# A hybrid encoder step in fp32: the embedding's input turned by VectorE ahead of time and kept in memory in two parts, and the embedding weight's parts kept too

## The chip, the cores and the metric

The kernel runs on one core of one Trainium2 chip. The metric is the device time of one execution in microseconds; lower is better. The engines named below are TensorE (PE in the profile: matmuls; PEld: its weight loads), VectorE (DVE), ScalarE (ACT), GpSimd (POOL) and SyncE (SP). SyncE computes nothing and issues most DMAs; GpSimd and ScalarE issue some as well. Each of these queues issues its DMAs in the order in which they stand in it.

## The reference, cut to what matters

One layer is applied to 2048 prompt rows and 32 sample rows of width 1024. First a mixer: RMSNorm, an input projection to 3072 columns, a short convolution and a pooling, and an output projection that is added to `h`. Then the per-layer embedding, which this change is about:

```python
    h = h + jnp.concatenate([yA, yB], axis=-1) @ w_out
    gate = jax.nn.sigmoid(rmsnorm(h, g_ple) @ w_ple_gate)
    h = h + (p @ w_ple) * gate
```

`p` is 2080 x 256 and `w_ple` 256 x 1024. A final RMSNorm closes the step. Everything is float32.

## The kernel before, in words

**Products in two parts.** A float32 operand is split by `split` (L77 to L80): ScalarE rounds it to the type fp32r (the high part, a CAST in the profile at L78) and VectorE subtracts that from the operand (the low part, L79). A product is then three matmuls: high by high, high by low, low by high. Most projections save one product in eight by Strassen's scheme on 2 x 2 blocks (`seven`).

**Stages.** The rows are cut into five blocks of 416, in three groups: blocks 0 and 1, 2 and 3, and block 4 with the 32 sample rows at its end.

1. The input projection runs over the groups (`GROUPS`), and in each over four units (j = 0 to 3; one unit has 128 channels of each kind). In the second group (profile: about 232 to 428 us) a unit is `Unit.seven`: 21 half products of 12 matmuls, each with weights that are loaded raw by SP, combined by VectorE and split by ScalarE and VectorE (`pair_weights`). Between the half products the unit calls `aside()`, 24 times in a unit. From unit 1 of the second group on, `aside` steps the generator `last_block`, which prepares the rows of the third group: SP loads them to a slot of the pool `xin` (five slots), VectorE scales them, POOL's queue stores them, SP loads them back in another order, VectorE turns them in 32 x 32 blocks in place (`turned_in_place`, L1112), and they are split and stored in `b_d` by POOL's queue. `at_pace(steps, num, den)` lets num of den calls of `aside` advance the generator by one step; `last_block` is stepped at 1 in 3.
2. At the end of the third group, `early_embedding` splits the embedding's weight (`embedding_weights`) and, after the group, the embedding's first three tiles (`EARLY`) are multiplied (about 540 to 549 us).
3. The output projection over pairs of 128-row tiles (about 549 to 711 us), with x added; `h` goes to memory (`h_d`).
4. The embedding `p @ w_ple` for the other tiles but one (about 711 to 751 us); its rows go to memory (`e_d`). Meanwhile the gate's weights are loaded (`wg_r`) and combined and split.
5. The gate projection over pairs of tiles (about 751 us to the end), with the product by the gate and the final norm. The last pair (`last_pair`) multiplies the embedding of the last tile itself.

**The embedding before the change.** Its input must stand with the 256 channels on the partitions. `embed` (L105 to L151) has `prep(c)` for tile c of its list and `run(c)`. For every fourth tile `prep` loads up to four tiles of `p` with one SP DMA (L122, sample rows L125). For each tile two TensorE transposes against the identity (L131) go to a PSUM bank, and `split` (L133) makes the parts `pps`. `run(c)` calls `prep` for c, c + 1 and c + 2, then does 12 matmuls of 512 columns (`embed_product`, L103), two ScalarE copies to the output tile (L148) and an SP store (L149). The slots of `pps` are four of the pool `st`, which the carried sums of the projections use as well. The weight's parts for stage 4 come from `embedding_chunks`: SP loads a chunk, ScalarE and VectorE split it into slots of the pool `cmb` (eight slots, shared with the frames of the output projection). `last_pair` does the same for its tile and weight (L1432, L1446).

**What sets the order.** The framework schedules: it walks the program with estimated costs and fixes each engine's and each queue's order; instructions with `keep_in_program_order` keep their place. On the chip each engine and each DMA queue then runs its list in order and waits on semaphores.

## Time and profile before

| | |
|---|---|
| median of 3 runs | 927.13 us (925.54 to 928.31) |
| profiled execution | 927.1 us |
| its span, first to last instruction | 925.3 us |
| TensorE busy | 907.0 us (98%), 4479 matmuls |
| VectorE busy | 722.8 us (78%) |
| ScalarE busy | 476.2 us (51%) |
| mean TensorE clock granted | 0.994 |
| moved by DMA | 186.37 MB, 201 GB/s over the span |

How to read the profile: a group line gives source line, engine, operation, output and inputs by the program's names, the shape, the count, then the busy time, the mean duration of one in ns, the idle time of the engine just before them and what ended it. A matmul's duration runs on into the next one, so the cost of a matmul on TensorE's path is the distance between starts. In the timeline a row gives the start and the length in us; rows of one kind that follow each other are merged and counted. "SPq" is SP's DMA queue.

### The profile page before, as it was taken

How to read it: one execution, taken by the hardware profiler on the slowest of the kernel's cores; microseconds unless marked ns; L12 is line 12 of the kernel's file. 1: busy time of each engine (PE TensorE's matmuls, PEld its weight loads, DVE VectorE, ACT ScalarE, POOL GpSimd, SP SyncE). 2: the span in 40 equal slices, each digit the busy share in tenths (PEclk: the TensorE clock that was granted, in tenths of full speed). 3: DMA queues.
4: the chain of work that ended last, by engine and by line, in shares of the span. 5: the costliest groups of instructions: out<-in, count | busy, mean ns of one | idle time of the engine just before them, and what ended most of it. 6: DMA issues, size and time to landing. Idle time of an engine off the chain costs nothing. (4 is left out here: it accounts for less than half of the span.)

```text
span 925.3 us, 12917 instructions
## 1 busy us (share of the span) xinstructions
PE 907.0 (98%) x4479; PEld 819.9 (89%) x4479; DVE 722.8 (78%) x1225; ACT 476.2 (51%) x880; POOL 152.8 (17%) x276
## 2 busy tenths in 40 slices
PE   7999999999999999999999999999999999999996
PEld 5999999999999999999999987888877868888884
DVE  6896898999488989785777679665554799888965
ACT  6744556554345455443545456334334776565554
POOL 3110222312001111000000010111111002333324
PEclk8999999999999999999999999999999999999998
DMA  8345555859955646357755359756775886799882
GB/s 245 87 152 153 167 160 178 265 154 317 411 165 174 191 155 189 100 180 277 201 169 173 125 192 289 263 186 177 251 220 167 292 259 160 190 232 232 227 240 91
DMA packets 140654, 186.37 MB, mean 201 GB/s; under 512 B 12044, under 2 KB 111244, under 8 KB 139309
## 3 DMA queue, kind: packets, MB, share of 16 engines
q1 hardware_dynamic: 120093, 126.07, 44.4%
q0 software_dynamic: 17760, 53.97, 19.8%
q10 hardware_dynamic: 2736, 5.51, 1.8%
q8 instruction: 35, 0.57, 0.3%
q14 instruction: 30, 0.25, 0.1%
HBM read 128.93 MB, written 56.56 MB: 200 GB/s over the span
## 5 line engine op out<-in xcount | busy, mean ns | idle before, releaser
L78 ACT CAST y_S<-y_fS 128x512 fp32r<-128x512 f32 x32 | 19.5, 621 | 41.9 <-PE x_o L168 18.9
L103 PE MATMUL e<-wq,pps 128*128 128x512 f32 (+1 forms) x156 | 38.9, 399 | 0.2 <-ACT pps L78 0.2
L168 PE MATMUL x_o<-wo_b,y_S 128*128 128x512 f32 x128 | 35.8, 391 | 0.0
L168 PE MATMUL x_g<-wg_b,g_S 128*128 128x512 f32 x128 | 35.7, 389 | 0.0
L564 PE MATMUL x_zbv<-B,w_zbv_S 128*128 128x416 f32 x168 | 34.2, 352 | 0.0
L564 PE MATMUL x_zab<-B,w_zab_S 128*128 128x416 f32 x168 | 34.1, 351 | 0.0
L564 PE MATMUL x_ch<-B,w_ch_S 128*128 128x416 f32 x168 | 34.1, 351 | 0.0
L564 PE MATMUL z_zab<-B,w_zab_S 128*128 128x416 f32 x168 | 34.0, 351 | 0.0
L564 PE MATMUL z_zbv<-B,w_zbv_S 128*128 128x416 f32 x168 | 34.0, 351 | 0.0
L564 PE MATMUL z_ch<-B,w_ch_S 128*128 128x416 f32 x168 | 34.0, 350 | 0.0
L103 PEld LDWEIGHTS e<-wq,pps 128*128 128x128 f32 (+1 forms) x156 | 27.4, 182 | 6.9 <-ACT pps L78 0.5
L1391 POOL DMA_DIRECT2D e<-h_d x28 | 24.8, 907 | 52.3 <-DVE e L1388 45.3
L70 POOL TENSOR_SCALAR ms_x<-ssq_x 128x1 f32<-128x1 f32 (+2 forms) x18 | 10.7, 592 | 127.5 <-ACT junk L89 127.2
L564 PEld LDWEIGHTS z_zbv<-B,w_zbv_S 128*128 128x128 f32 x168 | 31.4, 188 | 0.3
L564 PEld LDWEIGHTS z_zab<-B,w_zab_S 128*128 128x128 f32 x168 | 31.4, 188 | 0.3
L564 PEld LDWEIGHTS z_ch<-B,w_ch_S 128*128 128x128 f32 x168 | 31.4, 188 | 0.3
L564 PEld LDWEIGHTS x_zab<-B,w_zab_S 128*128 128x128 f32 x168 | 31.3, 188 | 0.4
L564 PEld LDWEIGHTS x_ch<-B,w_ch_S 128*128 128x128 f32 x168 | 31.3, 188 | 0.3
L564 PEld LDWEIGHTS x_zbv<-B,w_zbv_S 128*128 128x128 f32 x168 | 31.3, 188 | 0.4
L78 ACT CAST y<-y 128x512 fp32r<-128x512 f32 x24 | 14.8, 619 | 29.6 <-PE x_o L168 14.0
L168 PEld LDWEIGHTS x_o<-wo_b,y_S 128*128 128x128 f32 x128 | 23.9, 188 | 5.2 <-ACT c_o L1194 0.3
L168 PEld LDWEIGHTS x_g<-wg_b,g_S 128*128 128x128 f32 x128 | 24.0, 188 | 5.0
(582 smaller groups left out, 2649.9 us busy)
## 6 DMA issues: line engine op xcount, KB each, us to landing
y<-y_d SPq DMA_DIRECT2D x16, 512.0 KB, 6.3
x<-in_x_prompt_dram SPq DMA_DIRECT2D x16, 512.0 KB, 5.5
h_d<-x SPq DMA_DIRECT2D x16, 512.0 KB, 2.6
hn<-h_d SPq DMA_DIRECT2D x61, 128.0 KB, 6.7
xt<-in_x_prompt_dram SPq DMA_DIRECT2D x15, 512.0 KB, 7.4
e<-e_d SPq DMA_DIRECT2D x15, 512.0 KB, 5.9
e<-h_d POOLq DMA_DIRECT2D x28, 256.0 KB, 6.8
out_dram<-e POOLq DMA_DIRECT2D x14, 512.0 KB, 3.9
```

The lines of the kernel that those rows point to most:

```text
L70: nc.gpsimd.tensor_scalar(ms[:n], ssq[:n], scalar1=1.0 / D, scalar2=EPS, op0=ALU.mult, op1=ALU.add)
L78: ins = nc.scalar.copy(hi, src)
L103: nc.tensor.matmul(ps[:n], pps[:, a, k, :n], wp[k][b][:, cs], start=k + q == 0, stop=k == 1 and q == 2)
L168: nc.tensor.matmul(ps[:n], lhs[:, k, a, :n], w[b][:, k], start=start and k + q == 0, stop=k == KH - 1 and q == 2, skip_group_check=True)
L564: nc.tensor.matmul(ps[:, :NB], lhs[:, k, x], b[:, k, y], start=start and k + q == 0, stop=stop and k == KH - 1 and q == 2, skip_group_chec ...
L1391: nc.gpsimd.dma_start(ee, h_d[r:r + P, at[1] * NH:at[1] * NH + NH], accum_op=ALU.add)
```

## The change

The input `p` of the embedding is no longer turned by TensorE where it is used. A new generator, `p_steps`, does it in the second group, from unit 1 on, with the same means as `last_block`: SP loads four tiles in a block order (four DMAs, 64 channels each, in pieces of 256 bytes) to a slot of `xin`; VectorE turns them in place in 32 x 32 blocks; for each tile ScalarE and VectorE make the two parts, and POOL's queue stores them to `pt_d` (256 KB a tile). It is stepped at 23 in 68 calls of `aside`, beside `last_block`. Turning by blocks puts channels in another order on the partitions, so the rows of `w_ple` are loaded in the same order (four DMAs of 32 rows for each of two chunks). The weight's parts are stored once, at the end of the third group, to `wp_d`, and are loaded from there for stage 4 and the last pair; there they were split anew from the raw weight. `prep` in `embed` now only loads `pps` from `pt_d`, a tile at a time, and the transposes, the PSUM bank and the splits there are gone, in `last_pair` too.

```diff
+    pt_d = [tc.dram_tile([P, 2, 2, P], F32, name=f"pt_d{i}") for i in range(NT)]
+    wp_d = [[tc.dram_tile([P, D], F32, name=f"wp_d{k}{h}") for h in range(2)] for k in range(2)]
...
+    def p_load(pps, i):
+        n = tiles[i][1]
+        nc.sync.dma_start(pps.bitcast(F32)[:, :, :, :n], pt_d[i][:, :, :, :n])
...
-            pt = got["p"][:, (c % 4) * PLE:(c % 4 + 1) * PLE]
             pps = ring("pps", i)
-            ptp = tbank(f"ptp_{i}")
-            for k in range(2):
-                nc.tensor.transpose(ptp[:, k * P:k * P + n], pt[:n, k * P:(k + 1) * P], ident[:n, :n])
-            v = ptp.rearrange("p (k t) -> p k t", k=4)[:, :2, :n]
-            split(pps[:, 0, :, :n], pps[:, 1, :, :n], v)
+            p_load(pps, i)
...
-                nc.sync.dma_start(raw, w_ple[k * P:(k + 1) * P])
+                for q in range(4):
+                    nc.sync.dma_start(raw[q * 32:q * 32 + 32], w_ple[q * 64 + k * 32:q * 64 + k * 32 + 32])
                 t = [wtile(f"{name}{k}_{h}").rearrange("p k h n -> p (k h n)") for h in range(2)]
                 split(t[0], t[1], raw)
+                for h in range(2):
+                    nc.gpsimd.dma_start(wp_d[k][h], t[h].bitcast(F32))
...
+        def p_steps():
+
+            def load(c):
+                r, g = c * 4 * P, 16 if c < 4 else 1
+                t = ring4(xin, f"pc_{c}")[:, :g * 64]
+                for q in range(4):
+                    src = (p_p[r:r + 4 * P] if c < 4 else p_s)[:, q * 64:q * 64 + 64]
+                    nc.sync.dma_start(t[q * 32:q * 32 + 32].rearrange("p (g c) -> p g c", c=64),
+                                      src.rearrange("(g p) c -> p g c", p=32))
+                return t
+
+            t = load(0)
+            yield
+            for c in range(5):
+                tc.keep_in_program_order(nc.vector.transpose(t, t))
+                u = t.rearrange("p (g k t) -> p g k t", k=2, t=32)
+                yield
+                for m in range(4 if c < 4 else 1):
+                    i = c * 4 + m
+                    n = tiles[i][1]
+                    g = n // 32
+                    pps = pps_tile(i)
+                    v = lambda a: pps[:, a, :, :n].rearrange("p k (g t) -> p k g t", t=32)
+                    tc.keep_in_program_order(split(v(0), v(1), u[:, m * 4:m * 4 + g]))
+                    nc.gpsimd.dma_start(pt_d[i][:, :, :, :n], pps.bitcast(F32)[:, :, :, :n])
+                    if m == 0 and c < 4:
+                        t = load(c + 1)
+                    yield
...
-                        aside = at_pace(last_block(), 1, 3)
+                        paces = at_pace(last_block(), 1, 3), at_pace(p_steps(), 23, 68)
+                        aside = lambda: [pace() for pace in paces]
...
-        def embedding_chunks(name, rings=(ya, ya)):
+        def embedding_chunks(name):
...
-                raw = ring4(rings[k], f"{name}r_{k}")
-                nc.sync.dma_start(raw, w_ple[k * P:(k + 1) * P])
                 t = [cmb.tile([P, KH, 2, P], F32R, tag="c", name=f"{name}_{k}_{h}").rearrange("p a b c -> p (a b c)")
                      for h in range(2)]
-                split(t[0], t[1], raw)
+                for h in range(2):
+                    nc.sync.dma_start(t[h].bitcast(F32), wp_d[k][h])
...
-            pt = ss.tile([P, NH], F32, tag="s", name="p_l")[:, :PLE]
-            nc.sync.dma_start(pt, p_p[(i + 1) * P:(i + 2) * P])
+            pps = ss.tile([P, 2, 2, P], F32R, tag="s", name="pps_l")
+            p_load(pps, i + 1)
             e = load_rows(ya, "e", i, e_d)
-            wp = embedding_chunks("wl", (xh, qa))
+            wp = embedding_chunks("wl")
```

19 lines of the change are left out of this document (1 added, 18 removed).

## The prediction

> **What bounds the kernel now.** I read the page's engine line first, then the waits of TensorE, then windows by stage, then the timeline around the work that goes. The page and, under it, TensorE's waits (who, for whom, us in total, times, longest):
>
> ```profile
> PE 907.0 (98%) x4479; PEld 819.9 (89%) x4479; DVE 722.8 (78%) x1225; ACT 476.2 (51%) x880; POOL 152.8 (17%) x276
> ...
> PE pt L416 <- DVE xt L407: 3.2, 2, 2.3
> PE x_zab L564 <- DVE U L874: 0.3, 1, 0.3
> PE e L103 <- ACT pps L78: 0.2, 1, 0.2
> ```
>
> TensorE is busy 907.0 of 925.3 us, and its waits are small and mostly at the start. A matmul fewer is time gained, unless a neighbour becomes late. Which neighbour is near its limit is read by stage (length, busy time per engine with counts, clock, DMA share, GB/s): three units of the second group, the quiet end of the first projection, the embedding.
>
> ```profile
> 281.40:330.70 49.30, 49.01 (x260) 48.18 (x260) 43.68 (x78) 25.46 (x45) 7.32 (x11) 1.00 0.55 170
> 330.70:379.40 48.70, 48.70 (x259) 48.19 (x258) 44.80 (x75) 24.59 (x43) 5.78 (x7) 1.00 0.50 153
> 379.40:428.10 48.70, 48.70 (x259) 48.20 (x259) 36.19 (x60) 21.65 (x39) 2.89 (x4) 1.00 0.67 217
> 705.00:710.00 5.00, 5.00 (x24) 4.14 (x23) 1.38 (x2) 0.75 (x1) 0.00 (x0) 1.00 0.09 30
> 711.00:751.00 40.00, 39.76 (x190) 30.95 (x189) 28.59 (x52) 31.68 (x68) 1.06 (x3) 1.00 0.82 289
> ```
>
> The reader is to see that the change takes work from a stage whose second limit is DMA (0.82) and gives work to one whose second limit is VectorE (44.80 of 48.70 us).
>
> **What goes from TensorE.** There are 17 pairs of transposes, one pair a tile: 16 under L131, one under L1446. The groups and the timeline (start, length, engine, line, operation; in brackets the wait before it):
>
> ```profile
> L131 PE MATMUL ptp<-ident,ep 128*128 128x128 f32 (+1 forms) x32 | 5.7, 269 | 0.0
> ...
> 705.56 2.88 PE L168 MATMUL z_o<-wo_d,y_S 128*128 128x512 f32 x12
> 708.28 2.89 PE L168 MATMUL x_o<-wo_T,y 128*128 128x512 f32 x12
> 711.00 0.60 PE L131 MATMUL ptp<-ident,ep 128*128 128x128 f32 x4
> 711.84 0.96 PE L103 MATMUL e<-wq,pps 128*128 128x512 f32 x3 [0.24 <-ACT pps L78]
> 717.95 0.38 PE L131 MATMUL ptp<-ident,ep 128*128 128x128 f32 x2
> 718.08 3.00 PE L103 MATMUL e<-wq,pps 128*128 128x512 f32 x12
> 720.92 0.38 PE L131 MATMUL ptp<-ident,ep 128*128 128x128 f32 x2
> 721.06 3.00 PE L103 MATMUL e<-wq,pps 128*128 128x512 f32 x12
> ```
>
> A matmul's own duration overlaps the next one, so I go by starts. Twelve matmuls of 512 columns alone take 708.28 - 705.56 = 2.72 us. A tile of the embedding, twelve such and one pair, takes 721.06 - 718.08 = 2.98. A pair therefore costs 0.26 us of the path, and 17 pairs 4.4. At the start of the stage the four transposes and the wait for their copies take 711.84 - 711.00 = 0.84 us, of which two pairs are counted as 0.52; the other 0.3 goes too if the first tiles are there by 711. Gain: 4.7 us. Its bounds: 34 times the (0.60 - 0.27) / 3 = 0.11 between the starts of the four at 711.00 gives 3.7; 34 times the mean duration of 269 ns gives 9.1, excluded as an expectation by the 0.26 for a whole pair.
>
> On transposes the Trainium skill (TensorE: Matmul & The Clock Gate, Part 4: PE-mode transpose) gives about 275 ns in one kernel's context. By that as a cost on the path the gain would be an estimated 34 x 0.275 = 9.4 us; the trace agrees with it as a duration (269 ns), and not as a pitch.
>
> **What comes to the second group.** Five loads of 4 strided DMAs each on SP (20 issues), five VectorE transposes, 17 casts, 17 subtractions and 17 stores on POOL's queue, spread over 71 of the 72 steps of units 1 to 3. The nearest rows:
>
> ```profile
> L1112 DVE STREAM_TRANSPOSE xb<-xb x4: 433/1232/1234, 303.6 to 380.2; 128x1024 f32<-128x1024 f32 x3, 128x256 f32<-128x256 f32 x1
> L78 ACT CAST pps<-ptp 128x256 fp32r<-128x256 f32 (+1 forms) x16 | 5.7, 370 | 1.0 <-PE ptp L131 1.0
> L79 DVE TENSOR_TENSOR pps<-ptp,pps 128x256 fp32r<-128x256 f32 (+1 forms) x16 | 6.3, 407 | 3.2 <-ACT pps L78 3.1
> ...
> L1077 POOL DMA_DIRECT2D b_d<-b x8 | 7.2, 900 | 41.2 <-DVE U L704 23.7 <-DVE b L79 17.5
> ...
> 284.23 0.52 SPq L514 DMA_DIRECT2D raw_zab_1b<-in_w_in_dram  x1
> 292.52 0.69 DVE L542 TENSOR_TENSOR s_zab<-raw_zab_1b 128x512 f32<-128x512 f32 x1
> ...
> 354.66 1.27 DVE L79 TENSOR_TENSOR w_zab<-raw_zab_2a,w_zab 128x512 fp32r<-128x512 f32 x2
> 363.56 2.42 PE L564 MATMUL x_zab<-B,w_zab 128*128 128x416 f32 x12
> ```
>
> VectorE: 4 x 1.23 + 0.2 (a short one, below the 0.43 row) + 17 x 0.41 = 12.1 us, about 4.0 a unit. Idle there now: 49.30 - 43.68 = 5.6, then 48.70 - 44.80 = 3.9, then 12.5. The middle unit is filled to the brim, but its weights are parted 363.56 - 354.66 = 8.9 us before TensorE wants them; that lead covers a backlog of 8.0 (two units with none of their idle time usable), and the third unit pays it back. If the lead were gone, every us of backlog would be a us of TensorE. ScalarE gets 17 x 0.37 = 6.3 us, and is half idle there (24.59 of 48.70): nothing. POOL gets 17 issues of 0.90 us, 15.3 over three units in which it is busy for 16.0 of 146.7; a store that waits for its subtraction holds POOL's next root behind it, for which VectorE waits. SP's loads wait for one of xin's five slots, shared with the block of the third group, and raw weights queue behind them; one of these is issued 292.52 - 284.23 = 8.3 us before its first use, and a wait for a slot longer than that reaches VectorE. DMA: 17 tiles of 128 KB in and 256 KB out, 6.6 MB in 147 us, 45 GB/s on 153 to 217: nothing. What shows here today is one wait of 0.3 us (L564 for L874, above), in which TensorE needs a sum that VectorE takes late. I take +0.6 for more such; bounds -0.3 (that wait reshuffled away) and +3.0 (the 12.1 us as against the 8.9 of lead).
>
> At the end of the third group the weight's two loads become eight on SP, and four stores of its parts (512 KB each) go on POOL's queue. Nothing but the three early tiles follows them there, and these take other slots: nothing, bounds 0 and 0.5.
>
> **What comes to the embedding.** ScalarE and VectorE lose 13 pairs of parts (0.37 and 0.41 us) and the weight's parts; a tile's 128 KB in fours of SP loads becomes a load of both parts, 256 KB a tile, and the weight's 1 MB becomes 2 MB. Rows on landing (count, KB, median us), on SP's own waits, and on when the weight's slots open:
>
> ```profile
> hn<-h_d SPq DMA_DIRECT2D x61, 128.0 KB, 6.7
> e_d<-eout SPq DMA_DIRECT2D x12, 512.0 KB, 4.7
> wg_r<-g_d SPq DMA_DIRECT2D x8, 512.0 KB, 4.9
> ...
> SPq L149 <- ACT pps L78: 22.7, 9, 4.4
> ...
> L79 DVE TENSOR_TENSOR wq<-wqr,wq x2: 1217/1218/1218, 695.3 to 700.9; 128x1024 fp32r<-128x1024 f32 x2
> ```
>
> The weight: its last slot is written at 700.9, so it is open by then; a 512 KB load takes 4.9, so the last part is there at about 706, ahead of 711, in a stretch with DMA at 0.09. Nothing; if SP gets to it only behind the h_d stores after 711, up to 5 us.
> The tiles: a load may start when the fourth tile back is used up, 3 x 2.72 = 8.2 us before its own use; landing in 4.9 us it has 3.3 to spare for SP's queue, where the store of a finished tile stands in order and waits up to 4.4. DMA: ten tiles, 2.6 MB, come on top of 40 us x 289 GB/s = 11.6 MB; at 289 / 0.82 = 352 GB/s the 14.2 MB take 40 us, and the shortened stage has 37. Three us of stores must slip behind the stage, which the output slots allow for some tiles, but landings get longer, and the gate weights (ScalarE and VectorE already wait for wg_r) come through the same engines. I give back 1.2 of the 3.4 gained there; bounds 0 and 3.4 + 5.
> The Trainium skill (DMA: Bandwidth & Descriptors, Latency and other measured facts) has HBM access go from 0.2 us to 2 us at high load; by that a 4.9 us landing would be an estimated 6.7, still within 8.2. No run here shows it yet.
>
> **The last pair.** One pair less (in the 4.4). The wl parts' second write ends the slot wait, then 512 KB must land before the product:
>
> ```profile
> L79 DVE TENSOR_TENSOR wl<-wlr,wl x2: 1212/1215/1218, 897.1 to 902.7; 128x1024 fp32r<-128x1024 f32 x2
> 910.82 1.52 PE L103 MATMUL e_l<-wl,pps_l 128*128 128x512 f32 x6
> ```
>
> 902.7 + 4.9 = 907.6, 3.2 us to spare: nothing, bounds 0 and 3 (the loads of h behind it on SP).
>
> **Sum**, against the profiled execution's 927.1 us (span 925.3; the median of the runs is 927.13, so no shift): -4.7 + 0.6 + 1.2 = -2.9, or 924.2. A difference of 0.3%, 2.8 us, is about what can be told from none: 924.3 and 929.9.
>
> **Rivals.**
> 1. All the gain stays: 927.1 - 4.7 = 922.4. For it: 8.2 against 4.9 us, and the 8.9 of lead. Against: DMA over its limit.
> 2. The embedding becomes DMA's: 40 us for its 14.2 MB, as long as now; the early tiles and the last pair keep 4 x 0.26, plus 0.6 from the second group: 926.7. Between this and the forecast, 925.6 as its middle. For it: 0.82 and the waits for wg_r.
> 3. VectorE becomes the bound in units 1 and 2: +3.0 in place of +0.6: 926.4, or 927 with a second late sum.
> 4. Slower: the tile loads come late, in SP's queue. If queue and landing together take L, a tile takes L / 3 as soon as L is over 8.2. With hn's 6.7 and the mean SP wait (22.7 / 9 = 2.5), L is 9.2 and a tile 3.07, more than today's 2.98; with the longest wait, 4.4, L is 11.1, a tile 3.70 and 12 tiles +8.6, in all 927.1 + 8.6 - 1.0 + 0.6 = 935.3. It decides from L = 9.9. Against it: hn's landings are of 1 KB pieces elsewhere, and SP may get the loads ahead of the stores. Middle: 932.
> 5. A transpose costs its whole duration: 927.1 - 9.1 + 1.8 = 919.8. Against: the starts above.
>
> **Chances.** Forecast 0.42 (own range 922.8 to 925.2), rivals 0.15, 0.20, 0.09, 0.12, 0.02. Below 924.3 lie most of the forecast (0.31), rival 1, rival 5 and a little of 2: 0.50. Above 929.9 lie rival 4 and the worst of 2 and 3: 0.17. The rest, 0.33, is no change. Range 921.5 to 930.5: it leaves out rival 5 and a tail of 1, and most of 4.
>
> **What would show it.** Right: 34 matmuls fewer; tiles of the embedding 2.7 to 2.8 us apart by starts; VectorE at 47 to 48.7 us in the middle unit with TensorE's busy time still its length; the weight's loads issued before 706. Wrong: TensorE waiting on a DMA of pps (rival 4) or on wg parts after 745 (rival 2); waits for L874 or for weight parts between 281 and 428 (rival 3); SP holding the weight's loads behind h_d.

## The result, and the profile after

The changed kernel takes 961.72 us (median of 6 runs, 957.61 to 963.81), the kernel before 925.93 beside it (6 runs, 923.86 to 928.31): a ratio of 1.037, with a 95% interval of 1.0345 to 1.0395. The profiled execution took 960.51 us, with a span of 958.7 and a mean clock of 0.979 (before: 927.1, 925.3 and 0.994). It is slower by 3.7% where 0.3% faster was forecast.

The engine line of the page after, and TensorE's longest waits (us in all, times, longest):

```profile
PE 915.5 (95%) x4445; PEld 823.7 (86%) x4445; DVE 721.3 (75%) x1226; ACT 472.2 (49%) x876; POOL 168.4 (18%) x297
```

```profile
PE x_ch L555 <- ACT w_ch_S L80: 5.2, 1, 5.2
PE x_zbv L555 <- ACT w_zbv_S L80: 5.0, 1, 5.0
PE z_g L159 <- ACT c_g L1400: 3.8, 1, 3.8
PE pm L715 <- ACT pp L80: 3.3, 1, 3.3
PE x_gl L262 <- ACT wg_c L80: 2.8, 2, 2.3
```

The 34 matmuls are gone, and TensorE is busy for 8.5 us longer all the same: in the stretches with the long waits its granted clock is 0.87 to 0.90 (windows below). In place of waits of 0.2 and 0.3 us behind the start there are five places with some 3 to 5 us each: two in the middle unit of the second group, one in the last pair, one in the third group's first unit, and one at the seam between embedding and gate. I cut both traces at the first start of the product that opens each stage; the lengths in us:

| stage | before | after | difference |
|---|---|---|---|
| start, to the second group | 232.66 | 229.90 | -2.76 |
| second group, units 0 and 1 | 98.03 | 97.54 | -0.49 |
| second group, unit 2 | 48.73 | 64.28 | +15.55 |
| second group, unit 3 | 48.72 | 48.73 | 0 |
| third group, first unit | 27.87 | 35.10 | +7.23 |
| third group, the other units | 84.24 | 83.61 | -0.63 |
| early tiles and output projection | 171.59 | 172.54 | +0.95 |
| embedding (first `e` to first `x_gl`) | 39.40 | 37.09 | -2.31 |
| seam: the gate of the sample rows and of the first tile (to the first `x_g` with `wg_b`) | 15.53 | 26.16 | +10.63 |
| gate, to the last pair's `e_l` | 144.05 | 149.12 | +5.07 |
| end | 14.5 | 14.6 | +0.1 |
| span | 925.3 | 958.7 | +33.4 |

The four additions together are 38.5 us; the rest of the kernel is 5 us shorter. The windows of these stages after (length, busy time of PE, PEld, DVE, ACT and POOL with counts, clock, DMA share, GB/s): the middle unit of the second group (unit 2), the first unit of the third, embedding, seam:

```profile
327.44:391.72 64.28, 54.09 (x259) 52.16 (x259) 53.13 (x90) 27.71 (x54) 10.35 (x15) 0.89 0.71 194
440.45:475.55 35.10, 31.07 (x149) 29.51 (x149) 19.46 (x48) 13.10 (x26) 2.03 (x4) 0.90 0.82 264
731.70:768.79 37.09, 36.55 (x165) 28.69 (x164) 12.68 (x21) 22.23 (x42) 1.07 (x3) 1.00 0.96 336
768.79:794.95 26.16, 20.12 (x78) 12.52 (x77) 25.05 (x41) 16.98 (x32) 0.00 (x0) 0.87 0.68 213
```

Embedding and seam before:

```profile
711.84:751.24 39.40, 39.40 (x186) 30.73 (x187) 28.19 (x53) 31.49 (x67) 0.74 (x2) 1.00 0.83 292
751.24:766.77 15.53, 15.20 (x70) 9.93 (x68) 15.04 (x24) 11.63 (x21) 0.00 (x0) 1.00 0.66 201
```

**The middle unit.** VectorE is not full over the unit (53.13 of 64.28 us), so the time is lost at two places. SP's queue and then TensorE after:

```profile
294.60 0.39 SPq L505 DMA_DIRECT2D raw_zbv_2a<-in_w_in_dram  x1
307.78 2.42 SPq L1090 DMA_DIRECT2D pc<-in_p_prompt_dram  x4
...
328.72 0.44 SPq L505 DMA_DIRECT2D raw_zbv_2b<-in_w_in_dram  x1
...
336.56 2.68 SPq L1090 DMA_DIRECT2D pc<-in_p_prompt_dram  x4
...
343.39 0.47 SPq L505 DMA_DIRECT2D raw_ch_2b<-in_w_in_dram  x1
```

```profile
327.44 2.43 PE L555 MATMUL x_zbv<-B,w_zbv 128*128 128x416 f32 x12
329.71 2.43 PE L555 MATMUL y_zbv<-B,w_zbv 128*128 128x416 f32 x12
337.11 4.56 PE L555 MATMUL x_zbv<-B,w_zbv_S 128*128 128x416 f32 x12 [4.97 <-ACT w_zbv_S L80]
341.46 2.81 PE L555 MATMUL z_zbv<-B,w_zbv_S 128*128 128x416 f32 x12
...
360.83 4.56 PE L555 MATMUL x_ch<-B,w_ch_S 128*128 128x416 f32 x12 [5.22 <-ACT w_ch_S L80]
```

Before, the second half of this weight was issued 3.7 us after the first:

```profile
297.05 0.43 SPq L514 DMA_DIRECT2D raw_zbv_2a<-in_w_in_dram  x1
300.73 0.37 SPq L514 DMA_DIRECT2D raw_zbv_2b<-in_w_in_dram  x1
```

After, 34 us lie between them. SP's own waits from 290 to 346 us show why:

```profile
SPq L1090 <- DVE xs L1121: 12.7, 1, 12.7
SPq L1129 <- DVE pps L81: 7.3, 1, 7.3
SPq L1090 <- DMA xs_d<-xs: 6.5, 1, 6.5
SPq L708 <- DVE c_s L896: 6.5, 1, 6.5
```

The loads of the embedding's input (L1090) wait 12.7 us until VectorE has done with a slot. The next load of the third group's rows (L1129) then waits 7.3 us until VectorE has made parts out of a slot that the generator holds. The store of `c_s` behind it waits 6.5 us more, and only then does the second half go out, at 328.72. (The other 6.5 us of L1090 come later, ahead of `raw_ch_2b`.) The planner had put these DMAs between the two halves, so part of the 34 us is its order and not a slot.

The half lands 4.7 us after its issue. VectorE begins to combine it at 334.27, TensorE wants it at 332, and the whole lead of 8.9 us is gone. At the second place, `raw_ch_2b` goes out at 343.39, and VectorE takes it at 356.50, behind work that itself waits for the late products; which of the two holds it isn't settled. Of the 15.5 us, 10.2 are the two waits. Most of the rest is slow clock: the twelve products from 337.11 take 341.46 - 337.11 = 4.35 us, those from 327.44 take 2.27.

**The embedding and its seam.** The stage's own length came out as hoped: by starts a tile now takes 2.72 us. But the DMA engines' share is 0.96, and the gate's weights come late: the last of their eight loads goes out 45 us after the stage's first product, before 32. VectorE has 12.68 us of work during the embedding in place of 28.19, and 25.05 of 26.16 in the seam: the combining of the gate's weights has moved from under the embedding to behind it. One of VectorE's waits, and the time from issue to landing after (count, KB, median us):

```profile
742.77 0.69 DVE L169 TENSOR_TENSOR wg_r<-wg_r,wg_r 128x512 f32<-128x512 f32 x1 [10.18 <-DMA wg_r<-g_d]
```

```profile
e_d<-eout SPq DMA_DIRECT2D x12, 512.0 KB, 6.6
```

In the kernel before, the raw tiles were loaded ahead of the stage (the last of their loads for it at 696.55). After, ten of the 13 tile loads for this stage go out within it, up to 26.5 us behind its first product, since a tile's parts go into one of four slots each.

### The profile page after: what moved, and what is told of

The parts are those of the page before. It is cut to its first block, busy times and chain, and to the rows that moved or that the text cites. A ratio compares the mean times of both kernels' runs of the same rounds, so it can differ in the third digit from the quotient of the medians.

```text
span 958.7 us, 12951 instructions
## 1 busy us (share of the span) xinstructions
PE 915.5 (95%) x4445; PEld 823.7 (86%) x4445; DVE 721.3 (75%) x1226; ACT 472.2 (49%) x876; POOL 168.4 (18%) x297
## 5 line engine op out<-in xcount | busy, mean ns | idle before, releaser
L555 PE MATMUL x_ch<-B,w_ch_S 128*128 128x416 f32 x168 | 36.2, 367 | 5.2 <-ACT w_ch_S L80 5.2
L555 PE MATMUL x_zbv<-B,w_zbv_S 128*128 128x416 f32 x168 | 36.3, 367 | 5.0 <-ACT w_zbv_S L80 5.0
L555 PEld LDWEIGHTS x_ch<-B,w_ch_S 128*128 128x128 f32 x168 | 32.8, 198 | 6.2 <-ACT w_ch_S L80 5.6
L105 PE MATMUL e<-wq,pps 128*128 128x512 f32 (+1 forms) x156 | 36.2, 391 | 0.5 <-ACT ho L1374 0.5
L72 POOL TENSOR_SCALAR ms_x<-ssq_x 128x1 f32<-128x1 f32 (+2 forms) x18 | 14.0, 778 | 110.3 <-ACT junk L91 109.7
L159 PE MATMUL z_g<-wg_d,g_S 128*128 128x512 f32 x96 | 25.7, 421 | 3.8 <-ACT c_g L1400 3.8
```

The source lines that it names most:

```text
L72: nc.gpsimd.tensor_scalar(ms[:n], ssq[:n], scalar1=1.0 / D, scalar2=EPS, op0=ALU.mult, op1=ALU.add)
L105: nc.tensor.matmul(ps[:n], pps[:, a, k, :n], wp[k][b][:, cs], start=k + q == 0, stop=k == 1 and q == 2)
L159: nc.tensor.matmul(ps[:n], lhs[:, k, a, :n], w[b][:, k], start=start and k + q == 0, stop=k == KH - 1 and q == 2, skip_group_check=True)
L555: nc.tensor.matmul(ps[:, :NB], lhs[:, k, x], b[:, k, y], start=start and k + q == 0, stop=stop and k == KH - 1 and q == 2, skip_group_chec ...
```

## The experiments

The stage lengths of all runs, in us, cut as above; "E + S" is embedding and seam together.

| run | second group | third, first unit | E + S | gate | span | ratio to before (95%) |
|---|---|---|---|---|---|---|
| before | 195.48 | 27.87 | 54.93 | 144.05 | 925.3 | |
| after | 210.55 | 35.10 | 63.25 | 149.12 | 958.7 | 1.037 (1.0345 to 1.0395) |
| turn_alone | 209.93 | 34.99 | 54.09 | 145.33 | 946.3 | 1.0232 (1.0215 to 1.025) |
| load_alone | 195.49 | 27.87 | 63.41 | 145.85 | 943.7 | 1.023 (1.0201 to 1.0259) |
| weight_alone | 195.50 | 27.87 | 55.15 | 148.86 | 930.0 | 1.0054 (1.0037 to 1.0072) |
| weight_parted_anew | 210.90 | 35.22 | 65.60 | 151.91 | 965.1 | 1.0433 (1.0407 to 1.0459) |
| own_slot | 197.87 | 35.36 | 66.00 | 148.35 | 949.1 | 1.0272 (1.0242 to 1.0301) |
| own_early_store_on_act | 203.79 | 29.55 | 73.83 | 151.55 | 959.1 | 1.0381 (1.0351 to 1.0411) |
| own_early_tiles_on_pool | 204.97 | 29.52 | 72.48 | 153.56 | 966.8 | 1.047 (1.0441 to 1.0499) |
| tiles_on_pool | 210.01 | 35.01 | 56.43 | 156.65 | 964.1 | 1.0383 (1.0349 to 1.0417) |
| gate_weights_between | 211.27 | 35.44 | 63.47 | 154.50 | 966.1 | 1.0434 (1.041 to 1.0458) |
| before_gate_weights_between | 195.49 | 27.87 | 55.87 | 144.35 | 926.5 | 1.0012 (0.9998 to 1.0027) |
| turn_units_0_1 | 219.4 | 27.87 | 62.52 | 155.88 | 969.9 | 1.0511 (1.0479 to 1.0543) |
| turn_unit_0 | 228.0 | 27.87 | 68.10 | 152.46 | 983.1 | 1.0585 (1.054 to 1.0631) |
| one_part_kept | 211.36 | 27.88 | 51.47 | 158.46 | 950.7 | 1.0271 (1.0251 to 1.029) |
| turned_where_used | 195.49 | 27.88 | 73.54 | 156.16 | 955.5 | 1.0318 (1.0295 to 1.0341) |
| mended_early | 215.48 | 27.87 | 52.40 | 156.91 | 959.6 | 1.04 (1.0368 to 1.0433) |
| mended_late | 222.46 | 27.88 | 51.54 | 158.14 | 967.3 | 1.0474 (1.0447 to 1.0502) |

### The parts of the change, each alone

**turn_alone**: the kernel before, with `p_steps` beside `last_block`; what it stores is never read.

```diff
-                        aside = at_pace(last_block(), 1, 3)
+                        paces = at_pace(last_block(), 1, 3), at_pace(p_steps(), 23, 68)
+                        aside = lambda: [pace() for pace in paces]
```

> Here only the generator runs in the second group: it loads, turns, splits and stores the input's parts, and nobody reads them; the embedding, its weight and the last pair are as before. Theory A (the loss in the second group comes from the new work there, whatever is read later): the middle unit takes 15.5 us more as in the changed kernel (49 to about 64), and the first unit of the third group up to 7.2 more; embedding and last pair as before; about 939 to 949 us in all. Theory B (the second group is late only because later loads of the parts reorder the queues): the middle unit is 49 to 52 us, total 926 to 930.

Measured: second group +14.5 and third group +7.1, as in the changed kernel; embedding, seam and gate as before. TensorE has the same two waits of 5.2 and 5.0 us. The turning alone makes these two losses, as theory A has it.

**load_alone**: the changed kernel without `p_steps`; `pt_d` is filled by plain copies on POOL's queue instead, so its channels are not turned and the embedding's values are others.

```diff
-                        paces = at_pace(last_block(), 1, 3), at_pace(p_steps(), 23, 68)
-                        aside = lambda: [pace() for pace in paces]
+                        aside = at_pace(last_block(), 1, 3)
+                        for i, (r, n) in enumerate(tiles):
+                            for a in range(2):
...
+                                    nc.gpsimd.dma_start(v.rearrange("p k t -> p (k t)"), src)
```

> Here the generator does not run: the memory that the embedding reads is filled by plain copies from the input on GpSimd's queue early in the second group, so the channels are not turned and the embedding's values are others; the rest is the changed kernel, so the embedding and the last pair load parts of input and weight from memory. Theory A (losses are separate, by stage): second group as before (49 us a unit, within 2), embedding 3 us shorter, 9.5 us lost at the seam to the gate projection and 6.5 in the last pair: about 936 to 940 us. Theory B (the later losses only follow from the late second group): 920 to 926 us.

Measured: second and third group exactly as before, E + S 63.41 as in the changed kernel. So the seam's loss belongs to the loads from memory, not to the turning. The copies cost 10.3 us at the start (242.93 against 232.66), which the change itself doesn't have and which puts the total above the 936 to 940 of theory A.

**weight_alone**: the kernel before, with only the weight's parts kept and loaded.

```diff
+                for h in range(2):
+                    nc.gpsimd.dma_start(wp_d[k][h], t[h].bitcast(F32))
...
-                split(t[0], t[1], raw)
+                for h in range(2):
+                    nc.sync.dma_start(t[h].bitcast(F32), wp_d[k][h])
```

> The kernel before, with one part of the change: the embedding weight's parts are kept in memory and loaded for the embedding and the last pair; the input is turned by TensorE as before. Theory F (in the last pair four loads of parts wait for frame slots in SP's queue, with loads behind them that ScalarE needs): 3 to 6 us more in the last pair, 929 to 932. Rival (the last pair's loss belongs to the late gate weights before it): 924 to 927.

Measured: 0.5% slower, and every stage as before but the gate, with +4.8. TensorE in the last pair of this kernel (timeline):

```profile
909.82 4.36 PE L169 MATMUL z_g<-wg_d,g_S 128*128 128x512 f32 x12 [3.66 <-ACT c_g L1379]
```

Before, the same product starts after 0.21 us:

```profile
906.60 3.02 PE L168 MATMUL z_g<-wg_d,g_S 128*128 128x512 f32 x12 [0.21 <-ACT c_g L1377]
```

ScalarE frees a bank for this product late, since it first sums the squares of two blocks of rows `e`, and these come late. GpSimd's queue asks for the later one (`e<-h_d`) at 896.35; it lands after 10.4 us, and ScalarE goes on at 906.91. Meanwhile SP issues the four loads of the weight's parts (893.69 to 902.43), 2 MB; before, the raw weight's two loads had gone out long ahead. A window of 14 us (DMA share and GB/s at its end) and the median landing, in this kernel:

```profile
893.00:907.00 14.00, 13.16 (x59) 10.50 (x58) 5.08 (x8) 4.19 (x9) 3.87 (x5) 1.00 0.94 279
...
e<-h_d POOLq DMA_DIRECT2D x2, 256.0 KB, 9.6
```

Before:

```profile
890.00:904.00 14.00, 14.00 (x65) 11.53 (x64) 10.66 (x14) 7.20 (x13) 5.03 (x7) 1.00 0.67 177
...
e<-h_d POOLq DMA_DIRECT2D x3, 256.0 KB, 5.7
```

Theory F had the right time, but by SP's queue: nothing that ScalarE waits for here stands in it. own_early_store_on_act, below, loads the same parts behind `e<-h_d` on GpSimd's queue, and this product waits 0.21 us again. At the embedding itself the kept weight costs next to nothing (55.15 against 54.93).

**weight_parted_anew**: the changed kernel with the embedding weight loaded raw and split again for stage 4 and the last pair.

```diff
+                for q in range(4):
+                    nc.sync.dma_start(raw[q * 32:q * 32 + 32], w_ple[q * 64 + k * 32:q * 64 + k * 32 + 32])
...
-                for h in range(2):
-                    nc.sync.dma_start(t[h].bitcast(F32), wp_d[k][h])
+                split(t[0], t[1], raw)
```

> The changed kernel, but the embedding weight's parts are not kept in memory: for the embedding and the last pair they are split anew from the raw weight (loaded in the turned order of rows), as in the kernel before. Theory A (the loads of the weight's parts wait for frame slots and hold SP's queue): the 9.5 us at the seam to the gate projection and the 6.5 us of the last pair go; second group as changed; 944 to 948 us. Theory D (at the seam it is the loads of the input's parts, 256 KB a tile, between which the gate weights' loads stand in SP's queue): only the last pair's 6.5 us go, the seam keeps its loss; 953 to 957 us. Theory E (neither, the memory traffic as such): no change, 959 to 963.

Measured: the last pair's wait shrinks to 0.35 us, but E + S stays long (65.60) and the gate gets 2.8 us longer in another place: VectorE waits up to 5.4 us at a time for `hn` from `h_d`, loads that stand later in SP's new order. Undoing this part of the change gives no gain by itself, and the total is above all three forecasts.

### The middle unit: VectorE or SP's queue?

**own_slot**: `p_steps` gets a slot of its own, one tile at a time, so that its loads wait neither for `xin` nor hold it. VectorE's and ScalarE's work has the same elements. (This kernel computes wrong prompt rows, for a reason that the record doesn't show. Its generator's instructions are as many and of the same shapes as in the two `own_early` kernels, which compute the right rows and whose middle unit takes 49.5 and 49.2 us.)

```diff
+        pcs = frames_in.enter_context(tc.tile_pool(name="pcs", bufs=1, side="right"))
...
-                t = ring4(xin, f"pc_{c}")[:, :g * 64]
+                t = pcs.tile([P, PLE], F32, tag="t", name=f"pc_{i}")[:, :n * 2]
...
-                        paces = at_pace(last_block(), 1, 3), at_pace(p_steps(), 23, 68)
+                        paces = at_pace(last_block(), 1, 3), at_pace(p_steps(), 18, 70)
```

> The changed kernel, with the generator's loads taken out of the shared slots: one small slot of its own for one tile, a load for each tile (17 of 4 DMAs in place of 5), 17 shorter turns by VectorE; VectorE's and ScalarE's work is the same in elements, the rest as changed. Theory A (a load that waits for a shared slot holds SP's queue, and the next unit's raw weights behind it): the middle unit returns to 49 to 52 us and the first unit of the third group loses some of its 7.2 us; 939 to 947 us in all. Theory C (VectorE's 12 us of new work make it late): the middle unit stays at 58 us or more, 956 to 962 in all.

Measured: the middle unit is back at 48.83 us, with 45.78 us of VectorE's work in it. The window of this unit, and SP's longest wait from 290 to 346 us (total, times, longest):

```profile
330.30:379.13 48.83, 48.83 (x260) 48.09 (x259) 45.78 (x83) 25.05 (x49) 8.29 (x13) 1.00 0.67 201
...
SPq L1091 <- DVE pps L81: 15.9, 6, 4.8
```

This tells the two apart: VectorE holds the extra work at 45.8 of 48.8 us, and the shared slots, with SP's queue behind them, made the +15.5. SP still waits 15.9 us for the generator's own slot, but in six pieces of at most 4.8, and the two halves of the raw weight go out together again. So it isn't the sum of SP's waits that costs, but a long one ahead of a load that is needed soon. The edit changes the planner's order of SP's queue along with the waits, and the two aren't told apart. The second group gets 12.7 us shorter than in the changed kernel, the span only 9.6, since the third group's loss stays and E + S is 2.8 longer. In that third group VectorE waits in its order for the generator's last load:

```profile
435.87 0.24 DVE L1099 STREAM_TRANSPOSE pc<-pc 128x64 f32<-128x64 f32 x1 [9.55 <-DMA pc<-in_p_sample_dram]
```

### The seam of the groups

**own_early_store_on_act** steps `own_slot`'s generator faster, so that it ends before the group does, and puts the finished rows' stores on ScalarE's queue and the last pair's weight on POOL's.

```diff
+                        paces = at_pace(last_block(), 1, 3), at_pace(p_steps(), 18, 56)
...
+        _, run = embed(rest_e, wp, ring, nc.scalar)
...
+            wp = embedding_chunks("wl", nc.gpsimd)
```

> The changed kernel with four edits that lie in different stages: the generator's loads in one small slot of their own, a tile each; the generator stepped at 18 in 56 calls, so that it ends some 15 calls (about 30 us) before the second group does; in the embedding's stage ScalarE's queue issues the stores of finished tiles in place of SP's; in the last pair GpSimd's queue loads the weight's parts. Theory A: the middle unit is at 49 to 50 us and, as no load of the generator is under way at the seam to the third group, the third group's first unit returns from 35.1 to 28 to 29.5 us. Seam to the gate projection: if the stores' waits held the gate weights, 16 to 18 us; if the tile loads did, 23 to 27. Last pair: if SP's queue held it, 144 to 146 us from the first wg_b product to the last tile's embedding (before 144.1, changed 149.1); if any queue that waits there does, 147 or more. Total 921 to 928 with all four right, up to 940 if only the second group is.

Measured: the third group's first unit falls from 35.36 to 29.55, but the same wait for the generator's last load, here 6.3 us, now stands in the second group, whose last unit takes 53.75 us. E + S grows to 73.83, with a seam of 30.6 us, above what either theory for it said.

**own_early_tiles_on_pool** does the same with the tile loads on POOL's queue and the last pair's weight split anew.

```diff
+        _, run = embed(rest_e, wp, ring, nc.scalar, nc.gpsimd)
...
+            wp = embedding_chunks_raw("wl", (xh, qa))
```

> The changed kernel with the slot of its own and the faster pace (18 in 56), tile loads of the embedding's stage on GpSimd's queue and its stores on ScalarE's, and the last pair's weight split anew from the raw weight (the embedding's still from memory). Theory A for all stages: middle unit 49 to 50, third group's first unit 28 to 29.5, embedding 36 to 37.5, seam 15.5 to 18, from wg_b to the last tile's embedding 144 to 146: 919 to 924 us, below the kernel before. Rival (traffic sets the seam): seam 23 or more, 928 to 934.

Measured: 72.48 for E + S again. Here the row of VectorE's waits names the place: a gate weight's cast stands in ScalarE's order behind the copies of the embedding tiles.

```profile
DVE wg_d L81 <- ACT wg_c L80: 26.7, 2, 25.5
```

**turn_units_0_1** and **turn_unit_0** start the generator in unit 0 of the second group. Both also load the gate's weights between the tiles (as in gate_weights_between, below), split the last pair's weight anew and load each chunk of the embedding's weight with one DMA.

```diff
+                    if j == 0:
+                        turning, rest_of = at_pace(p_steps(), 23, 44), aside
+                        aside = lambda: [pace() for pace in (rest_of, turning)]
```

(turn_unit_0 has `at_pace(p_steps(), 1, 1)` there.)

> The changed kernel, mended in four places: the generator starts with unit 0 of the second group and is done in 44 of its calls of aside (units 0 and 1, where VectorE has 15.9 of 48.7 us and 5.6 of 49.3 idle before), still in the shared slots; the gate weights' pieces stand between the embedding's tiles; the last pair's weight is split anew; a chunk of the embedding's weight comes in one DMA of turned rows in place of four. Theory A: units 0 and 1 together 98 to 101 us (before 98.0), unit 2 and 3 at 49 each, third group's first unit 28 to 29, embedding 37 to 39.5, seam 14 to 18, from wg_b to the last tile 144 to 146; total 919 to 926. Rival (VectorE's 12 us of work are paid wherever they stand): units 0 and 1 together 105 or more, total 930 or more.

> As the one with the generator in units 0 and 1, but a step with every call of aside, so that all of it is in unit 0, before the third group's rows use the shared slots. Theory A (it is the sharing of slots and of SP's queue with the third group's rows that costs): units 0 and 1 together 98 to 99.5 us, units 2 and 3 at 48.7 as before, third group 28, the rest as there; total 917 to 923. Rival (DMA: 6.6 MB in 48.7 us are 136 GB/s on top of 274, against some 352 at most): unit 0 takes up to 8 us more, 925 to 931.

Measured: the third group's first unit is at 27.87 in both, exactly as before, so its +7.2 comes from the generator's tail. (The third group's last unit, though, takes some 5 us more in both, as in the two mended kernels below; why isn't known.) But the second group is worse, 219.4 and 228.0. The first half of unit 0 before:

```profile
232.66:260.00 27.34, 27.34 (x146) 27.06 (x146) 11.80 (x23) 9.66 (x18) 0.54 (x1) 1.00 1.03 397
```

Over the whole of unit 0 VectorE has 32.8 us of work in 48.7, which is why I tried it; but in its first half the DMA engines are already full (1.03). In turn_unit_0 the generator's first loads stand ahead of the raw weight `raw_ch_0b`, which goes out at 219.89, before at 211.51. It lands only as the large loads of the group's rows end: VectorE waits 25.5 us for it, until 255.98, and TensorE 18.1 us for VectorE. (Before, a weight that went out at 222.85 landed at 255.86 too, but nobody on TensorE's path needed it by then.)

### The embedding: order, queue or bytes?

**tiles_on_pool** puts the tile loads on POOL's queue.

```diff
-        nc.sync.dma_start(pps.bitcast(F32)[:, :, :, :n], pt_d[i][:, :, :, :n])
+        queue.dma_start(pps.bitcast(F32)[:, :, :, :n], pt_d[i][:, :, :, :n])
...
+        _, run = embed(rest_e, wp, ring, loads=nc.gpsimd)
```

> The changed kernel; only the queue of one load is other: in the embedding's stage GpSimd's queue, idle there, issues the loads of the input's parts in place of SP's. Theory D (the gate weights' loads stand in SP's queue behind tile loads that wait for slots): from the first gate product to the first with the weight part wg_b it takes 16 to 18 us again in place of 26.2 (before: 15.5), total 950 to 954. Rival (the engines' traffic: 256 KB a tile in place of 128, whatever queue issues it): stays at 25 or more, total 960 to 963. Second and third group stay as in the changed kernel.

Measured: the gate's weights are in time again (the last load 33 us after the stage's first product, before 32, in the changed kernel 45), and the seam takes 13.15 us, with the same bytes as in the changed kernel. So the tile loads in SP's queue do hold the gate's weights, as theory D has it. But the embedding takes 43.28, the stretch ahead of it 4.1 us more, since the first tile comes 4.8 us late, and the gate 7.5 more. Of the 6.8 us that E + S falls, to 56.43, 2.7 are left after the 4.1.

**gate_weights_between** and **before_gate_weights_between** put one of the gate weight's pieces in the program ahead of every second tile of the embedding, in the changed kernel and in the kernel before.

```diff
+        pieces = iter(range(KH))
+        for c in range(len(rest_e) - LATE):
+            if c >= 0 and (c - 0) % 2 == 0:
+                for k in [next(pieces, None)]:
+                    if k is not None:
+                        wg_piece(k)
+            run(c)
```

> The changed kernel; only the place in the program is other at which the gate's weights are loaded, combined and split: four pieces, written ahead of the first, third, fifth and seventh tile of the embedding's stage in place of behind all its tiles. Theory D (the order of SP's queue, made by the planner, holds the gate weights): from the first gate product to the first with wg_b 14 to 18 us in place of 26.2, the embedding 37 to 39.5, total 950 to 954; second group, third group and last pair stay as in the changed kernel. Rival (memory traffic in that stage): 25 or more at the seam, 959 to 963.

> A control: the kernel before, with the gate weights' pieces written between the embedding's tiles, nothing else. If the order of the pieces matters only where tile loads hold SP's queue: no change, 924 to 928. If it is a gain of its own: 3 us or more off, and what a mended version gains is not the change's.

Measured: without the change the order makes no difference (1.0012). With it the seam falls from 26.16 to 14.09 and the embedding grows from 37.09 to 49.38: TensorE now waits 4.4 us for tiles. The sum, 63.47, is that of the changed kernel. A window of this embedding:

```profile
735.00:765.00 30.00, 23.56 (x87) 17.48 (x86) 17.91 (x28) 19.25 (x36) 0.74 (x2) 0.83 0.86 306
```

Here too the gate's weights are in time and the tiles late: in these two runs another order changes who waits, and E + S does not come back to 54.9.

**one_part_kept** keeps the turned tiles undivided: 128 KB a tile in place of 256, as many loads; the two parts are made where they are used.

```diff
-        nc.sync.dma_start(pps.bitcast(F32)[:, :, :, :n], pt_d[i][:, :, :, :n])
+        t = t[:, :n * 2]
+        nc.sync.dma_start(t, pt_d["t"][:, i * PLE:i * PLE + n * 2])
+        v = lambda a: pps[:, a, :, :n].rearrange("p k (g t) -> p g k t", t=32)
+        split(v(0), v(1), t.rearrange("p (g k t) -> p g k t", k=2, t=32))
```

> The changed kernel, but the turned input is kept in memory unsplit: 128 KB a tile in place of 256, stored straight from the slot where VectorE turned it (5 stores, no splits in the second group), and split into its parts by ScalarE and VectorE where it is used, as in the kernel before; the tile loads are as many and in SP's queue as before. Theory G (the DMA engines are full in the embedding's stage, share 0.97 to 0.99, and the 1.7 MB more of tile loads push the gate weights or the tiles behind): from the embedding's first product to the first with wg_b 53 to 57 us in place of 63.3. Theory D (the number and order of loads in SP's queue): 61 to 64. In the second group a slot is free as soon as it is stored: if the length for which a chunk holds its shared slot makes the middle unit's loss, it falls from 64 to 49 to 54 us; if the loads themselves do, it stays at 60 or more. Total 938 to 950 by the first of each.

Measured: E + S 51.47, that is 11.8 below the changed kernel and 3.5 below the kernel before: here is the gain that was forecast. The window of its embedding:

```profile
726.18:762.43 36.25, 36.25 (x165) 28.77 (x164) 25.53 (x47) 29.80 (x62) 1.33 (x3) 1.00 0.87 304
```

The DMA share is 0.87 in place of 0.96, and the loss is gone. But more than the bytes is other here. An undivided tile goes into a slot of another pool (`ya`), four tiles to a slot, and so all 13 tile loads go out 47 to 36 us ahead of the stage's first product at 726.18. The last nine:

```profile
685.52 4.92 SPq L110 DMA_DIRECT2D ep<-pt_d  x9
```

The last of the gate's weights goes out 31 us after that product, in the changed kernel 45. So the run shows that the loss goes when no tile load falls into the stage. Whether half the bytes at the same place in SP's queue would have done it is not shown.

In the second group the run met neither forecast: units 1 and 2 together take 113.8 us, in the changed kernel 113.1, before 98.0. VectorE makes no parts there and has only the five turns to do, so the loss doesn't need its work. The gate takes 158.46 us, which gives the embedding's gain back (below).

**turned_where_used** does without memory for the tiles: the kernel before, with four strided loads and a VectorE transpose where the TensorE transposes stood.

```diff
-            for k in range(2):
-                nc.tensor.transpose(ptp[:, k * P:k * P + n], pt[:n, k * P:(k + 1) * P], ident[:n, :n])
...
+                w = pt[:, :len(full) * PLE + (m - len(full)) * 64]
+                nc.vector.transpose(w, w)
...
+            p_split(pps, pt, n)
```

> The kernel before, with the transposes moved from TensorE to VectorE in the embedding itself: the input is loaded in the block order (four DMAs in place of one for four tiles), turned in place by VectorE and split; nothing of the change's memory, no work in the second group; the weight's rows are loaded in the turned order. The 34 matmuls go as in the changed kernel. Theory: second and third group, seam and last pair as before (97 to 99, 48.7, 48.7, 27.9; 15.5; 144), the embedding 36.5 to 38 in place of 39.4 and the early tiles 0.5 shorter: 921 to 924 us. Rival: pieces of 256 bytes make the loads slow (DMA share 0.80 to 0.88 there now), TensorE or VectorE waits for them: 926 to 932.

Measured: groups as before, and the same 186.37 MB as the kernel before, but E + S is 73.54. Here it is SP's order: the tiles' loads stand between stores of finished rows, three of which take 5.8 us, and the first of the eight gate weights goes out as late as 738.23 (before, the last had left by 744.26).

```profile
728.41 5.75 SPq L155 DMA_DIRECT2D e_d<-eout  x3
734.21 2.16 SPq L107 DMA_DIRECT2D ep<-in_p_sample_dram  x4
...
738.23 0.43 SPq L1344 DMA_DIRECT2D wg_r<-g_d  x1
```

So the loss at the seam can come from SP's order alone, with no byte more. In the changed kernel it comes from the tile loads that fall into the stage (load_alone, one_part_kept); how much of it is their place in SP's queue and how much their bytes is not settled.

### Two attempts at a better kernel

**mended_early** and **mended_late** join what had helped: undivided tiles, turned from unit 0 on with loads on POOL's queue, the weights split anew as before. They differ by a delay of 5 and of 10 calls in the generator.

```diff
+            ts = [load(c) for c in range(2)]
+            for _ in range(5):
+                yield
+            for c in range(5):
+                tc.keep_in_program_order(nc.vector.transpose(ts[c], ts[c]))
+                nc.gpsimd.dma_start(pt_d[:, c * D:c * D + (D if c < 4 else 64)], ts[c])
+                if len(ts) < 5:
+                    ts.append(load(len(ts)))
```

> All causes taken away at once. The generator runs in unit 0 of the second group, before the third group's rows use the shared slots; GpSimd's queue issues its 20 loads and 5 stores in place of SP's; it keeps the turned input unsplit (128 KB a tile, as much as the raw input), loaded by fours as in the kernel before and split at use; the weight is split anew as before (its rows in the turned order). A chunk is turned 5 calls of aside (about 10 us) or more behind its load. Theory: units 0 and 1 at 98 to 101 us, units 2 and 3 at 48.7, third group's first unit 27.9, embedding and seam together 51.5 to 53 (before 54.9), from wg_b to the last tile 143.5 to 145: 920 to 924.5 us. Rival (a further cause in the second group, such as VectorE's queue waiting for a chunk's load): units 0 and 1 at 103 or more, 928 to 940.

> The same with each chunk turned 10 calls of aside (about 20 us) or more behind its load. If VectorE's wait for a load is what is left, units 0 and 1 are shorter than in the run with 5 calls, 98 to 100 us, and the total 920 to 924. If the shared slots' late return to the third group's rows is, unit 1 and 2 show it instead: units 0 and 1 or unit 2 longer by 2 us or more, 925 to 930.

Measured: third group 27.87 and 27.88, E + S 52.40 and 51.54, both as wanted; but the second group +20 and +27, and the gate +13 and +14. In unit 0 TensorE waits for a raw weight that lands 37.2 us after its issue, before 33.0 (mended_early):

```profile
260.13 3.86 PE L569 MATMUL x_zab<-B,w_zab 128*128 128x416 f32 x11 [9.87 <-ACT w_zab L79]
```

The landing is 4 us later; the rest is order. Here the product stands next after those that end at 250 us; before, all but one of its matmuls stood at 264.58, behind other products.

In the gate VectorE stands for 7.6 us at the split of the last tile's parts. No version ran faster than the kernel before.

## Why the prediction was wrong, by its steps

**What goes from TensorE: right where it was read.** 34 matmuls fewer, tiles 2.72 us apart, the embedding 2.3 us shorter. With the seam, one_part_kept shows 3.5 us of gain; the whole 4.7 no run shows.

**What comes to the second group: this step failed.** It had the mechanism in words (loads wait for one of five slots, raw weights queue behind them, a wait longer than 8.3 us reaches VectorE) and then took +0.6, with an upper bound of 3.0 from VectorE's work against the lead of the weights. That bound priced the wrong queue. Twenty more issues for the same five slots were never counted as a wait of SP's. A wait of 12.7 us came, above the 8.3 that the prediction itself had named, and one of 7.3 behind it; the lead of 8.9 went, and the unit got 15.5 us longer. With a slot of its own, and no single wait for it over 4.8, the unit lost 0.1 and the whole group 2.4. Rival 3, a full VectorE, falls by the same run. (Its 926.4 is 926.6 by the prediction's own terms.) That the slow clock adds to each wait was in no bound: in this unit it makes up to a third of the loss.

**The seam of the groups: in no step.** At the end of the third group the prediction took nothing, and nothing came there (the other units -0.63). But the group's first unit took 7.2 us more. The prediction had spread the generator over 71 of 72 steps and not asked what its last steps meet: it ends at the seam of the groups. SP's loads for what follows (`y`, `x`, `wo_q`) go out between 432 and 443 us, before between 390 and 395. The output projection's weight `wo_r` comes behind them, at 447.76, and VectorE, which works in order, stands 7.4 us for it:

```profile
447.76 1.07 SPq L991 DMA_DIRECT2D wo_r<-in_w_out_dram  x2
```

```profile
455.32 0.69 DVE L169 TENSOR_TENSOR wo_r<-wo_r 128x512 f32<-128x512 f32 x1 [7.44 <-DMA wo_r<-in_w_out_dram]
```

Before, the first of these two loads went out at 427.45. What VectorE makes next is needed for the pooling, and TensorE waits 3.3 us for that. A second, smaller way is the one that the prediction had named for another stage and at no price ("a store that waits ... holds POOL's next root"): on POOL's queue half of the rows that open the group stands behind a store that waits 2.7 us for VectorE, and TensorE waits 0.7 us for these rows. The five runs whose last store goes out 25 us or more before the group ends have 27.87 or 27.88. Which of the two moves comes from the generator's tail itself, and which from the planner's new order with it, isn't told apart.

**What comes to the embedding: the direction was right, the size wrong.** The prediction had the DMA share over its limit (14.2 MB in 37 us at 352 GB/s) and expected stores to slip. 12.46 MB were moved in these 37 us. It gave back 1.2 us, with 3.4 + 5 as the worst; 10.6 came. The term that was mis-sized is what the late loads cost. Not the tiles were late but the gate weights, and behind each of them stand pieces of 0.7 us of VectorE's and ScalarE's work; VectorE's busy time in the seam went from 15.0 to 25.1 us, and the difference had been hidden under the embedding. Rival 2 had named the gate weights, but priced them at the stage's own length, which came to nearly nothing; it says that full DMA engines hold them, while tiles_on_pool speaks for the tile loads' place in SP's queue; how much the DMA engines add, the runs leave open. Rival 4, tiles late in SP's queue, didn't happen: TensorE waits for no tile in the changed kernel. The Trainium skill (DMA: Bandwidth & Descriptors, Latency and other measured facts) was cited with access to HBM going from 0.2 to 2 us at high load, an estimated 6.7 for a landing of 4.9. The stores of the finished rows went from 4.7 to 6.6 with the DMA share at 0.96, which agrees in size; the tiles' own loads landed in 4.5.

The sign that the weight's loads are issued early held, counted from the stage: the last goes out at 721.01, 10.7 us ahead of the stage's first product at 731.70 (the 706 was 5.8 us ahead of 711.84). The kept weight did no harm there (weight_alone: 55.15 against 54.93).

**The last pair: bound too low.** Nothing was taken, 3 was the bound, 4.8 came (weight_alone). The step had asked when the first product needs the weight, not what else the DMA engines carry meanwhile: the rows `e` landed after 9.6 us in place of 5.7, and ScalarE and then TensorE waited for them.

**What was in no step.** The start and units 0 and 1 got 3.2 us shorter, the third group's last unit 4 to 5 us longer in four runs, and the gate stage took 144 to 158 us over the runs, though no line of it changed in many of them. An edit elsewhere made the planner set another order. In the gate of one_part_kept and of the mended kernels this took back the whole gain of the embedding. Which single move in the order does it is not settled.

## What to carry to other kernels

Before a load is added to a queue that runs in order, ask whose slot it must wait for and what stands behind it, and compare the longest such wait with the lead of what stands behind: 12.7 us against a lead of 8.9 cost 15.5, six waits of at most 4.8 cost 0.1. It can't be read from any engine's busy share. When a stage is near its DMA limit, look at what loads an edit moves into it, and price the next stage's work coming out from under cover, not the stage's own length. And where a planner orders the rest, an edit that gains 3 us must first get past reorderings that cost 5 to 15.

## What the runs showed of the hardware

**A wait of TensorE costs more than itself.** The pitch of matmuls is the distance between their starts. In the changed kernel's last pair twelve products of 512 columns take 942.35 - 937.07 = 5.28 us after a wait of 3.78, a mean pitch of 440 ns (426 to 427 from the second on), while those from 929.04 took 2.72, 227 ns each:

```profile
929.04 2.88 PE L159 MATMUL z_g<-wg_a,g_S 128*128 128x512 f32 x12
931.76 1.52 PE L159 MATMUL x_g<-wg_b,g_S 128*128 128x512 f32 x6
937.07 5.49 PE L159 MATMUL z_g<-wg_d,g_S 128*128 128x512 f32 x12 [3.78 <-ACT c_g L1400]
942.35 1.88 PE L159 MATMUL x_g<-wg_b,g_S 128*128 128x512 f32 x6
```

Whether it comes isn't decided by the length of the wait alone. The same product in load_alone kept its pace after 3.19 us (2.86 us for twelve), while in weight_parted_anew a product of the gate lost it after 2.19, from its fifth matmul on (4.44 for twelve):

```profile
925.78 3.02 PE L159 MATMUL z_g<-wg_d,g_S 128*128 128x512 f32 x12 [3.19 <-ACT c_g L1378]
928.64 1.52 PE L159 MATMUL x_g<-wg_b,g_S 128*128 128x512 f32 x6
```

```profile
910.20 4.60 PE L158 MATMUL x_g<-wg_T,g 128*128 128x512 f32 x12 [2.19 <-DVE c_g L1407]
914.64 1.52 PE L158 MATMUL x_g<-wg_c,g 128*128 128x512 f32 x6
```

The Trainium skill (TensorE: Matmul & The Clock Gate, Part 1) has the clock halve after an idle window of about 3.4 us that runs freely, and a pitch of 426.7 ns for 512 columns then. The pitch agrees, and 3.19 us without a loss are shorter than such a window; but so are the 2.19 us, behind which the loss came.

**The DMA engines' limit** shows at 397 GB/s in the first half of unit 0 before (share 1.03), where 8.35 of 10.85 MB come in 711 packets, and at 336 in the changed kernel's embedding (0.96), with 12.46 MB in 5065 packets. Whether the size of the pieces or the mix of loads and stores makes the difference is not shown.
